# A convolution kernel's first step: stream sums on TensorE, a reordered set-up, and a split last store

## The chip, the cores and the metric

The kernel runs on one core of one Trainium2 chip. The metric is the device time of one execution in microseconds (us). The profile's span is about 2 us shorter than that time.

## The reference

A causal convolution over time with eight taps, each a full 512 x 512 matrix:

```python
x: (8, 4096, 512), kernel: (8, 512, 512)
for k in range(8):
    shifted = x moved k steps later in time, zeros in front
    out += np.matmul(shifted, kernel[k])
```

## The kernel before

Each of the 128 partitions owns a run of 256 consecutive time steps. A step of the kernel handles eight of them, so there are 32 steps. Within a step the eight taps are combined by a three-level scheme of sums and differences, which needs 27 matrix products in place of 64: three nodes (LO, HI, MID) of nine products each. A product is four accumulating matmuls of 128 x 128 by 128 x 512. The scheme needs

- **streams**: sums of x rows at several distances (`D4`, `D42`, `D421`, `D41`, and `F1`, `F2`, `F21` for the very first step), which are the stationary operands, and
- **weight differences** (`mid_a`, `mid_b`, `mid_c`): 19 combinations of the eight taps, 128 x 2048 each, made once. A product can start only when its weight is there.

The first step also needs the **history**: the seven rows ahead of each run, which belong to the neighbouring partition. Before the change the set-up was:

```python
    nc.vector.memset(D421, 0.0)
    xi = [load_x(0, 0)]                       # first half of x, step 0
    for b in range(B):                        # history, 8 pieces of 15 partitions
        nc.gpsimd.dma_start(out=D421[b*G+1:(b+1)*G, 1:8], in_=xr[...])
    for tap in (6, 4, 7, 5): load_w(tap)
    xi.append(load_x(0, 1))                   # second half of x, step 0
    for tap in (2, 0, 3, 1): load_w(tap)
    ...
        transpose_pe(T, xi[0], range(0, 4))   # TensorE, then ScalarE copies to XT
        transpose_pe(H, D421, range(0, 8))    # history
        tt(D4[:, 5:8], H[:, 1:4], hs[:, 1:4], ADD)      # VectorE makes all sums
        tt(D4[:, 0:4], hs, XT[:, 0:4], ADD)
        ...                                   # five weight differences
        transpose_pe(T, xi[1], range(4, 8))   # ahead of every product
        ...                                   # F1, F2, F21, the HI streams
    for k in range(4): ...                    # matmuls of zero into the four bank pairs
```

Every node then runs `node_a1` (one product and a ScalarE copy), `node_a0u` (two products), `node_seed` (ScalarE copies that seed the output banks), `node_v` (two products with VectorE's combination), four times `node_l` (the last products) and `node_e` (the output). In these traces each engine takes its work in the order of the program; e2 shows it for TensorE, with a wait of 4.0 us.

## Time and profile before

| | before |
|---|---|
| device time, median of 3 | 796.1 us |
| span of the profile | 793.6 us |
| TensorE busy | 760.0 us |
| VectorE's first sum | 18.4 us |
| first product on TensorE | 32.3 us |
| first `node_l` of node 2 on TensorE | 62.6 us |
| last matmul ends | 788.7 us |

The row that matters most is the last but one. From there to the end TensorE is full in both kernels (the last matmul ends 726.0 us later before the change, 726.1 us after it), so all that the change can win at the start is how much earlier that product comes. I call this instant **the marker**: in the timeline of TensorE it is the group of `F` matmuls which follows the four with `D` that are node 3's first product. In the kernel before it is the second of these lines (start, duration, engine; `x8` counts the matmuls; the bracket is the wait ahead of the group and what ended it):

```profile
61.42 1.03 PE L217 MATMUL qq<-w,D 128*128 128x512 bf16 x4
62.63 1.89 PE L217 MATMUL pp<-w,F 128*128 128x512 bf16 x8 [0.18 <-DVE pp L82]
```

The other lines behind the table stand in the prediction below.

### The profile page before, as it was taken

How to read it: one execution, taken by the hardware profiler on the slowest of the kernel's cores; microseconds unless marked ns; L12 is line 12 of the kernel's file. 1: busy time of each engine (PE TensorE's matmuls, PEld its weight loads, DVE VectorE, ACT ScalarE, POOL GpSimd, SP SyncE). 2: the span in 40 equal slices, each digit the busy share in tenths (PEclk: the TensorE clock that was granted, in tenths of full speed). 3: DMA queues.
4: the chain of work that ended last, by engine and by line, in shares of the span. 5: the costliest groups of instructions: out<-in, count | busy, mean ns of one | idle time of the engine just before them, and what ended most of it. 6: DMA issues, size and time to landing. Idle time of an engine off the chain costs nothing.

```text
span 793.6 us, 9335 instructions
## 1 busy us (share of the span) xinstructions
PE 760.0 (96%) x3528; PEld 345.7 (44%) x3528; DVE 662.3 (83%) x762; ACT 277.6 (35%) x455; POOL 44.7 (6%) x86
## 2 busy tenths in 40 slices
PE   2579999999999999999999999999999999999997
PEld 2224444444444444444444444444444444444443
DVE  1989898888888888889888888988888879888895
ACT  2233323333333333333333333333333333333332
POOL 6000000000000000000000000000000000000000
PEclk9999999999999999999999999999999999999999
DMA  9936777787878778778878877787778777878842
GB/s 153 209 52 177 186 173 178 169 203 167 206 160 188 170 175 183 188 172 189 192 164 176 188 193 169 182 176 176 175 188 207 156 190 171 174 188 184 192 137 121
DMA packets 161132, 138.83 MB, mean 175 GB/s; under 512 B 132296, under 2 KB 136392, under 8 KB 161088
## 3 DMA queue, kind: packets, MB, share of 16 engines
q1 hardware_dynamic: 147392, 99.63, 46.1%
q0 software_dynamic: 13696, 38.61, 30.4%
q8 instruction: 27, 0.44, 0.2%
q14 instruction: 17, 0.14, 0.1%
HBM read 77.22 MB, written 67.11 MB: 182 GB/s over the span
## 4 chain that ended last, share of the span: by engine, by line
PE 94%; DMA 2%; DVE 2%; ACT 1%; issue 0%; POOL 0%; ACTq 0%
PE pp L217 62%; PE qq L217 31%; DMA xin<-in_x_dram 2%; DVE w L82 1%; DMA D<-in_x_dram 1%; POOL w L143 0%; PE pp L208 0%; PE xt L167 0%; ACT XT L188 0%; DVE D L135 0%; ACT pp L259 0%; DVE y L82 0%; ACT qq L247 0%; PE qq L208 0%; DVE pp L271 0%
## 5 line engine op out<-in xcount | busy, mean ns | idle before, releaser
L217 PE MATMUL pp<-w,D 128*128 128x512 bf16 x2280 | 523.4, 379 | 1.4 <-ACT pp L259 1.3
L217 PEld LDWEIGHTS <-D 128*128 128x128 bf16 x3296 | 322.5, 98 | 394.5 <-issue 6.5
L217 PE MATMUL qq<-w,D 128*128 128x512 bf16 x1016 | 251.2, 380 | 1.4 <-ACT qq L247 1.4
L82 DVE TENSOR_TENSOR D<-D 128x1024 bf16<-128x1024 bf16 (+1 forms) x256 | 232.0, 947 | 0.1
L82 DVE TENSOR_TENSOR y<-pp,ms 128x1024 f32<-128x1024 f32 x124 | 151.4, 1221 | 47.9 <-PE pp L217 47.9
L82 DVE TENSOR_TENSOR D<-XT 128x2048 bf16<-128x2048 bf16 (+2 forms) x157 | 146.6, 950 | 7.6 <-DMA XT<-xin 6.3
L247 ACT COPY qq<-qq 128x512 f32<-128x512 f32 x96 | 54.7, 570 | 267.3 <-PE qq L217 267.3
L259 ACT COPY pp<-qq 128x512 f32<-128x512 f32 x96 | 54.7, 570 | 177.1 <-PE qq L217 172.7
L82 DVE TENSOR_TENSOR pp<-dts,pp 128x512 f32<-128x512 f32 x96 | 66.4, 692 | 51.5 <-ACT dts L263 47.2
L294 ACT COPY ms<-pp 128x1024 f32<-128x1024 f32 x62 | 63.0, 1016 | 34.2 <-PE pp L217 34.2
L87 POOL DMA_DIRECT2D xin<-in_x_dram x64 | 34.0, 532 | 699.0 <-DMA XT<-xin 688.1
L271 DVE SCALAR_TENSOR_TENSOR pp<-pp,dts 128x512 f32<-128x512 f32 x96 | 66.8, 695 | 3.6
L263 ACT COPY dts<-qq 128x512 f32<-128x512 f32 x96 | 58.2, 606 | 0.0
L261 ACT ACTIVATE pp<-qq 128x512 f32<-128x512 f32 x96 | 56.6, 590 | 0.1
L217 PE MATMUL qq<-w,XT 128*128 128x512 bf16 x124 | 31.8, 379 | 0.0
L82 DVE TENSOR_TENSOR w<-w,w 128x2048 bf16<-128x2048 bf16 x19 | 22.4, 1219 | 0.2
L167 PE MATMUL xt<-ident,xin 128*128 128x128 bf16 x32 | 3.8, 312 | 15.4 <-DMA xin<-in_x_dram 15.4
L217 PEld LDWEIGHTS <-XT 128*128 128x128 bf16 x124 | 12.1, 98 | 14.6
L82 DVE TENSOR_TENSOR D<-hist,D 128x1536 bf16<-128x1536 bf16 x1 | 1.0, 957 | 15.1 <-ACT D L175 15.1
L167 PEld LDWEIGHTS <-xin 128*128 128x128 bf16 x32 | 3.2, 146 | 15.7 <-DMA xin<-in_x_dram 15.7
L167 PE MATMUL hist<-ident,D 128*128 128x128 bf16 x32 | 3.8, 313 | 4.1 <-DMA D<-in_x_dram 4.1
L217 PEld LDWEIGHTS <-F 128*128 128x128 bf16 x36 | 3.3, 97 | 9.5 <-DVE w L82 4.8
(28 smaller groups left out, 51.4 us busy)
## 6 DMA issues: line engine op xcount, KB each, us to landing
out_dram<-y SPq DMA_DIRECT2D x128, 512.0 KB, 3.3
xin<-in_x_dram POOLq DMA_DIRECT2D x64, 512.0 KB, 6.0
w<-in_kernel_dram POOLq DMA_DIRECT2D x8, 512.0 KB, 13.9
XT<-xin SPq DMA_TRANSPOSE x62, 6.1
D<-in_x_dram POOLq DMA_DIRECT2D x8, 105.0 KB, 5.1
```

The source lines that it names most:

```text
L82: nc.vector.tensor_tensor(out=o, in0=a, in1=b, op=op)
L87: nc.gpsimd.dma_start(out=xin, in_=xr[:, K * i + 4 * h:K * i + 4 * h + 4, :])
L167: nc.tensor.transpose(o[:, t, c * P:(c + 1) * P], src[:, t % src.shape[1], c * P:(c + 1) * P], ident)
L217: nc.tensor.matmul(bank, lhsT=comp[:, c * P:(c + 1) * P], rhs=w[:, c, :], start=start and c == 0, stop=c == DC - 1, skip_group_check=True)
L247: nc.scalar.copy(out=n.q[:, 0], in_=n.q[:, 1])
L259: nc.scalar.copy(out=n.p[b_][:, 1], in_=n.q[:, 1])
L261: nc.scalar.mul(out=n.p[b_][:, 1], in_=n.q[:, 1], mul=-1.0)
L263: nc.scalar.copy(out=n.dts, in_=n.q[:, 0])
L271: nc.vector.scalar_tensor_tensor(out=p[:, 0], in0=p[:, 1], scalar=-1.0, in1=n.dts, op0=MUL, op1=SUB)
L294: nc.scalar.copy(out=ms[b_], in_=p)
```

## The change

The intent: let products begin before the second half of x has landed; take sums off VectorE by letting TensorE add while it transposes (two matmuls with an identity into one bank); take two weight differences off VectorE (one matmul with the identity, one with its negative); release TensorE's clock early with matmuls on zero (in the kernel before its matmuls take 0.43 us each until 34.2 us, then 0.216); load the history in two large transfers; and finish the last output pair in halves, stored from two queues. Cut to its core:

```diff
-    nc.vector.memset(D421, 0.0)
-    xi = [load_x(0, 0)]
-    for b in range(B): ... 15 rows of history each
+    nc.gpsimd.dma_start(out=H[1:P, 4:8], in_=xr[0:P - 1, RUN - 4:RUN, :])
+    x0 = [load_x(0, 0)]
+    nc.gpsimd.dma_start(out=H[1:P, 1:4], in_=xr[0:P - 1, RUN - 7:RUN - 4, :])
+    make_identity(nc, ident)          # also identh (batch starts zeroed), identn (negative)
+    nc.vector.memset(H[0:1], 0.0)
...
+    for r in range(2):
+        for k in range(4):
+            fill(pair(k))             # 16 matmuls on zero
+    o = transpose_pe(x0[0], 0)
+    nc.scalar.copy(out=XT[:, 0:4], in_=o)
+    pw = sums_pe(1, (-4, 0), (-3, 1))
+    nc.vector.tensor_copy(out=D4[:, 0:2], in_=pw)
...                                   # the other D4 parts, F1, F2, F21 in the same way
     nodes = [node_a1(0)]
     node_a0u(nodes[0])
     node_seed(nodes[0])
+    o = transpose_pe(x0[1], 2)        # second half of x only here
     node_v(nodes[0], 0)
     node_v(nodes[0], 1)
...
+                by_pe(*mid_a(LO, HI), (2, 0))
...
+                by_pe(*mid_a(HI, HI), (1, 0))
...
+            if b_ == HI and n.k == len(order) - 1:
+                for j, eng in enumerate((nc.scalar, nc.sync)):
+                    tt(y[:, j], p[:, j], ms[b_][:, j], ADD if n.a == LO else SUB)
+                    eng.dma_start(out=orr[:, ... + j, :], in_=y[:, j])
```

More of the change, by code (lines that the diff above doesn't have):

```diff
@@ L54 @@
     ctx.enter_context(tc.manual_schedule())
-    ident = spool.tile([P, P], bf, name="ident")
-    make_identity(nc, ident)
-    zero = spool.tile([P, D], bf, name="zero")
-    nc.vector.memset(zero, 0.0)
     W = {}
@@ L74 @@
     D1 = spool.tile([P, 2, D], bf, name="D1")
-    F2 = spool.tile([P, 5, D], bf, name="F2")
+    F2 = spool.tile([P, 2, D], bf, name="F2")
     F21 = spool.tile([P, 4, D], bf, name="F21")
@@ L131, in prep_d421, with pair @@
             tt(D421[:, 4:8], D42[:, 3:7], D42[:, 4:8], ADD)
-    nc.vector.memset(D421, 0.0)
-    xi = [load_x(0, 0)]
-    for b in range(B):
-        nc.gpsimd.dma_start(out=D421[b * G + 1:(b + 1) * G, 1:8],
-                            in_=xr[b * G:(b + 1) * G - 1, RUN - 7:RUN, :])
+    ppool = ctx.enter_context(tc.tile_pool(name="p", bufs=1, space=PSUM))
+    def pair(k):
+        return ppool.tile([P, 2, D], f32, name=f"pp{k}")
+    H = D421
+    nc.gpsimd.dma_start(out=H[1:P, 4:8], in_=xr[0:P - 1, RUN - 4:RUN, :])
+    x0 = [load_x(0, 0)]
+    nc.gpsimd.dma_start(out=H[1:P, 1:4], in_=xr[0:P - 1, RUN - 7:RUN - 4, :])
+    ident = spool.tile([P, P], bf, name="ident")
+    make_identity(nc, ident)
+    identh = spool.tile([P, P], bf, name="identh")
+    nc.gpsimd.tensor_copy(out=identh, in_=ident)
+    nc.gpsimd.memset(identh[:, 0:P:G], 0.0)
+    identn = spool.tile([P, P], bf, name="identn")
+    nc.gpsimd.tensor_scalar_mul(out=identn, in0=ident, scalar1=-1.0)
+    zero = spool.tile([P, D], bf, name="zero")
+    nc.vector.memset(zero, 0.0)
+    nc.vector.memset(H[0:1], 0.0)
     def load_w(tap):
@@ L145, in mid_a, with by_dve, by_pe @@
     def mid_a(b_, c_):
-        tt(W[MID, b_, c_], W[HI, b_, c_], W[LO, b_, c_], SUB)
+        return W[MID, b_, c_], W[HI, b_, c_], W[LO, b_, c_]
     def mid_b(a, c_):
-        tt(W[a, MID, c_], W[a, HI, c_], W[a, LO, c_], SUB)
+        return W[a, MID, c_], W[a, HI, c_], W[a, LO, c_]
     def mid_c(a, b_):
-        tt(W[a, b_, MID], W[a, b_, LO], W[a, b_, HI], SUB)
+        return W[a, b_, MID], W[a, b_, LO], W[a, b_, HI]
+    def by_dve(o, u, v):
+        tt(o, u, v, SUB)
+    def by_pe(o, u, v, prs):
+        for h in range(2):
+            pw = pair(prs[h])
+            for k in range(2):
+                nc.tensor.matmul(pw[:, k], lhsT=ident, rhs=u[:, 2 * h + k], start=True, stop=False)
+                nc.tensor.matmul(pw[:, k], lhsT=identn, rhs=v[:, 2 * h + k], start=False, stop=True)
+            nc.scalar.copy(out=o[:, 2 * h:2 * h + 2], in_=pw)
@@ L154 @@
     for tap in (6, 4, 7, 5):
         load_w(tap)
-    xi.append(load_x(0, 1))
+    x0.append(load_x(0, 1))
     for tap in (2, 0, 3, 1):
         load_w(tap)
-    with tc.tile_pool(name="t", bufs=1, space=PSUM) as tpool:
-        H = tpool.tile([P, K, D], bf, name="hist")
-        T = tpool.tile([P, K, D], bf, name="xt0")
-        def transpose_pe(o, src, ts_):
-            for t in ts_:
-                for c in range(DC):
-                    nc.tensor.transpose(o[:, t, c * P:(c + 1) * P],
-                                        src[:, t % src.shape[1], c * P:(c + 1) * P], ident)
-        transpose_pe(T, xi[0], range(0, 4))
-        transpose_pe(H, D421, range(0, 8))
-        nc.scalar.copy(out=XT[:, 0:4], in_=T[:, 0:4])
-        nc.scalar.copy(out=F0, in_=T[:, 0])
-        hs = D421[:, 4:8]
-        nc.scalar.copy(out=hs, in_=H[:, 4:8])
-        tt(D4[:, 5:8], H[:, 1:4], hs[:, 1:4], ADD)
-        tt(D4[:, 0:4], hs, XT[:, 0:4], ADD)
-        prep_d41(LO)
-        mid_b(LO, HI)
-        tt(D42[:, 7], D4[:, 5], D4[:, 7], ADD)
-        prep_d42(LO)
-        mid_c(LO, LO)
-        prep_d421(LO)
-        mid_b(LO, LO)
-        mid_c(LO, MID)
-        mid_c(LO, HI)
-        transpose_pe(T, xi[1], range(4, 8))
-        nc.scalar.copy(out=XT[:, 4:8], in_=T[:, 4:8])
-        tt(F1[:, 0], hs[:, 3], XT[:, 0], ADD)
-        tt(F1[:, 1], XT[:, 0], XT[:, 1], ADD)
-        tt(F2[:, 0], hs[:, 1], hs[:, 3], ADD)
-        tt(F2[:, 1:3], hs[:, 2:4], XT[:, 0:2], ADD)
-        tt(F2[:, 3:5], XT[:, 0:2], XT[:, 2:4], ADD)
-        tt(F21, F2[:, 0:4], F2[:, 1:5], ADD)
-        prep_d4(HI)
-        prep_d41(HI)
-        prep_d42(HI)
-        prep_d421(HI)
-        prep_d27()
@@ L200, with fill, transpose_pe @@
-    xi = [load_x(1, 0), load_x(1, 1)]
-    ppool = ctx.enter_context(tc.tile_pool(name="p", bufs=3, space=PSUM))
-    qpool = ctx.enter_context(tc.tile_pool(name="q", bufs=1, space=PSUM))
-    for k in range(4):
-        pw = ppool.tile([P, 2, D], f32, name="pp") if k else qpool.tile([P, 2, D], f32, name="qq")
+    def fill(pw):
         for h in range(2):
             nc.tensor.matmul(pw[:, h], lhsT=ident, rhs=zero, start=True, stop=True)
+    def transpose_pe(src, k):
+        o = pair(k).bitcast(bf).rearrange("p a (b d) -> p (a b) d", b=2)
+        for t in range(4):
+            for c in range(DC):
+                nc.tensor.transpose(o[:, t, c * P:(c + 1) * P], src[:, t, c * P:(c + 1) * P], ident)
+        return o
@@ new lines, in x_at, with sums_pe @@
+    def x_at(t):
+        return (x0[0][:, t], ident) if t >= 0 else (H[:, 8 + t], identh)
+    def sums_pe(k, *sums):
+        pw = pair(k)
+        for h, ts_ in enumerate(sums):
+            for c in range(DC):
+                for n, t in enumerate(ts_):
+                    src, idt = x_at(t)
+                    nc.tensor.matmul(pw[:, h, c * P:(c + 1) * P], lhsT=src[:, c * P:(c + 1) * P],
+                                     rhs=idt, start=n == 0, stop=n == len(ts_) - 1,
+                                     skip_group_check=True)
+        return pw
@@ new lines @@
+    for r in range(2):
[5 more added lines that the diff above has]
+    nc.vector.tensor_copy(out=D4[:, 0:2], in_=pw)
+    pw = sums_pe(2, (-2, 2), (-1, 3))
+    nc.vector.tensor_copy(out=D4[:, 2:4], in_=pw)
+    pw = sums_pe(3, (-5, -1))
+    nc.vector.tensor_copy(out=D4[:, 7], in_=pw[:, 0])
+    pw = sums_pe(0, (-7, -3), (-6, -2))
+    nc.scalar.copy(out=D4[:, 5:7], in_=pw)
@@ new lines @@
+    prep_d41(LO)
+    pw = sums_pe(1, (-1, 0), (0, 1))
+    nc.scalar.copy(out=F1, in_=pw)
+    fill(pair(3))
+    tt(D42[:, 7], D4[:, 5], D4[:, 7], ADD)
+    prep_d42(LO)
+    pw = sums_pe(2, (-2, 0), (0, 2))
+    nc.scalar.copy(out=F2, in_=pw)
+    pw = sums_pe(0, (-3, -2, -1, 0), (-2, -1, 0, 1))
+    nc.scalar.copy(out=F21[:, 0:2], in_=pw)
+    by_dve(*mid_b(LO, HI))
+    pw = sums_pe(1, (-1, 0, 1, 2), (0, 1, 2, 3))
+    nc.scalar.copy(out=F21[:, 2:4], in_=pw)
+    nc.scalar.copy(out=F0, in_=XT[:, 0])
@@ L210 @@
+    fill(pair(0))
+    fill(pair(1))
+    prep_d421(LO)
+    by_dve(*mid_c(LO, LO))
+    by_dve(*mid_b(LO, LO))
+    by_dve(*mid_c(LO, MID))
+    by_dve(*mid_c(LO, HI))
+    xi = [load_x(1, 0)]
     mpool = ctx.enter_context(tc.tile_pool(name="m", bufs=2))
@@ L226, in streams @@
         if a == MID and i == 0:
-            return (F0, [F1[:, 0], F1[:, 1]], [F2[:, 1], F2[:, 3]],
+            return (F0, [F1[:, 0], F1[:, 1]], [F2[:, 0], F2[:, 1]],
                     [F21[:, j] for j in range(4)])
@@ L234, in streams, with node_a1 @@
                 [D421[:, o + j] for j in range(4)])
-    def node_a1(i, a):
+    def node_a1(k):
         n = Node()
-        n.i, n.a, n.s = i, a, streams(i, a)
-        n.q = qpool.tile([P, 2, D], f32, name="qq")
+        n.k, (n.i, n.a) = k, order[k]
+        a = n.a
+        n.s = streams(n.i, a)
+        n.q = pair(3)
         product(n.q[:, 1], n.s[1][1], W[a, MID, HI], True)
@@ L256, in node_seed @@
         for b_ in range(2):
-            n.p[b_] = ppool.tile([P, 2, D], f32, name="pp")
+            n.p[b_] = pair((2 * n.k + b_) % 3)
             if b_ == LO:
@@ L296, in node_e @@
             y = ypool.tile([P, 2, D], f32, name="y")
-            if n.i == 0:
+            if b_ == HI and n.k == len(order) - 1:
+                for j, eng in enumerate((nc.scalar, nc.sync)):
+                    tt(y[:, j], p[:, j], ms[b_][:, j], ADD if n.a == LO else SUB)
+                    eng.dma_start(out=orr[:, K * n.i + 4 * n.a + 2 * b_ + j, :], in_=y[:, j])
+            elif n.i == 0:
                 nc.scalar.copy(out=y, in_=p)
@@ L306 @@
     order += [(i, a) for i in range(1, NIT) for a in (MID, LO, HI)]
-    nodes = [node_a1(*order[0])]
+    nodes = [node_a1(0)]
     node_a0u(nodes[0])
     node_seed(nodes[0])
+    o = transpose_pe(x0[1], 2)
     node_v(nodes[0], 0)
     node_v(nodes[0], 1)
+    nc.scalar.copy(out=XT[:, 4:8], in_=o)
+    xi.append(load_x(1, 1))
+    prep_d4(HI)
+    prep_d41(HI)
+    by_dve(*mid_b(HI, HI))
+    prep_d42(HI)
     for k, (i, a) in enumerate(order):
@@ L324 @@
             if k == 0:
-                mid_b(HI, HI)
-                mid_c(HI, LO)
-                mid_b(HI, LO)
-                mid_c(HI, MID)
-                mid_c(HI, HI)
-                nodes.append(node_a1(*order[1]))
-            else:
-                mid_a(LO, HI)
-                mid_a(HI, HI)
-                mid_b(MID, HI)
-                mid_a(LO, LO)
-                mid_a(HI, LO)
-                mid_b(MID, LO)
-                mid_c(MID, MID)
-                mid_c(MID, LO)
-                mid_c(MID, HI)
-                nodes.append(node_a1(*order[2]))
-            node_e(cur, 1)
+                by_pe(*mid_a(LO, HI), (2, 0))
+                node_e(cur, 1)
+                fill(pair(2))
+                nodes.append(node_a1(1))
+                by_pe(*mid_a(HI, HI), (1, 0))
+                prep_d421(HI)
+                by_dve(*mid_b(HI, LO))
+                by_dve(*mid_c(HI, MID))
+                by_dve(*mid_c(HI, LO))
+                by_dve(*mid_c(HI, HI))
+                by_dve(*mid_b(MID, HI))
+                by_dve(*mid_a(LO, LO))
+                prep_d27()
+            else:
+                by_dve(*mid_a(HI, LO))
+                by_dve(*mid_b(MID, LO))
+                by_dve(*mid_c(MID, MID))
+                by_dve(*mid_c(MID, LO))
+                by_dve(*mid_c(MID, HI))
+                nodes.append(node_a1(2))
+                node_e(cur, 1)
         nxt = nodes[k + 1] if k + 1 < len(order) else None
@@ L374 @@
             node_l(cur, 1, HI)
-        if 1 <= k and k + 2 < len(order):
-            nodes.append(node_a1(*order[k + 2]))
+        if k and k + 2 < len(order):
+            nodes.append(node_a1(k + 2))
         if k >= 2:
```

## The prediction

> **What bounds the kernel now.** I read the page's busy shares and groups first, then the chain that ended last, then the timeline of the first 70 us and the last 15 us. The page says where the bulk lies:
>
> ```profile
> PE 760.0 (96%) x3528; PEld 345.7 (44%) x3528; DVE 662.3 (83%) x762; ACT 277.6 (35%) x455; POOL 44.7 (6%) x86
> PE   2579999999999999999999999999999999999997
> L217 PE MATMUL pp<-w,D 128*128 128x512 bf16 x2280 | 523.4, 379 | 1.4 <-ACT pp L259 1.3
> ```
>
> TensorE is full from the fourth slice (each is 19.8 us) to the end; 1.4 us of idle in 2280 matmuls. A busy mean of 379 ns counts overlap: 1391 matmuls start in the 300 us from 100 to 400, so one costs 0.2157 us. There are 96 nodes x 9 products x 4 = 3456 of them: 745.5 us at that pace. The last ends at 788.66, so 43.2 us are lost before and between, nearly all at the start. The change leaves the 3456 alone; it can win only part of those 43 us and of the 4.9 us after 788.66. The chain over the first 70 us, start and duration ahead of each piece:
>
> ```profile
> 7.97 0.78 POOL w L143
> ...
> 11.14 13.86 DMA xin<-in_x_dram
> 25.00 0.05 issue
> 25.05 1.90 PE xt L167 x16
> ...
> 28.89 1.01 PE qq L208 x2
> 29.90 2.56 PE pp L208 x6
> 32.46 1.72 PE qq L217 x4
> ...
> 49.65 2.27 DVE w L82 x2
> 51.92 0.02 issue
> 51.95 3.51 DVE w L82 x3
> ...
> 61.89 0.70 DVE pp L82
> ```
>
> The reader sees that no product starts before 32.3 us, because the second half of the first x tile (landed 25.0) is transposed ahead of all products, and that from 49 us TensorE waits for VectorE's weight differences. The four matmuls from 32.46 take 0.43 us each, twice 0.2157; from 34.87 they run at full pace. The page's clock row does not show this. VectorE in that stretch (start, duration, engine):
>
> ```profile
> 18.41 0.96 DVE L82 TENSOR_TENSOR D<-hist,D 128x1536 bf16<-128x1536 bf16 x1 [15.13 <-ACT D L175]
> 39.95 5.88 DVE L82 TENSOR_TENSOR w<-w,w 128x2048 bf16<-128x2048 bf16 x5
> 49.56 10.67 DVE L82 TENSOR_TENSOR w<-w,w 128x2048 bf16<-128x2048 bf16 x9
> ```
>
> It idles 15.1 us, starts at 18.4 and then runs to 62.6 with about 4 us of gaps: some 40 us of work. **The start is a VectorE chain that begins late**; at 62.63 TensorE takes over as bound.
>
> **The skill.** "TensorE: Matmul & The Clock Gate", Part 1, says the array starts at half clock and is released after about 3.4 us of sustained work (free-running window); the trace agrees in kind: 0.43 us a matmul until 34.2, after 5.3 us of matmuls, then 0.216. Part 4 of that page says transposes do not count as busy for the gate, and Part 2 gives about 81 ns for a sustained N=128 load-and-matmul pair; the trace only has the slow ones, 16 transposes in 1.90 us. "VectorE: DVE Perf Modes", the perf-mode tier table: a bf16 tensor_tensor of 2048 takes 1224 ns, which the trace shows (1.22), and an fp32 PSUM operand drops to 1x, which 1.22 us for 1024 elements of the y additions shows. "DMA: Bandwidth & Descriptors", Issuing engines are not separate DMA queues: a second queue saves only issue time.
>
> **Part 1, loads.** The history goes from eight 15-row transfers behind a 1.76 us memset to two of 127 rows issued first. The queue then moves 0.52 MB at about 2.4 us (0.524 MB at 218 GB/s, as between 18 and 34 us). Before, the weight taps landed near 15.2, 18.0, then some 2.35 us apart, x half two at 25.0. After, I estimate x half one 8.0, second history 9.8, taps 12.2, 14.6, 17.0, 19.4, x half two 21.8, taps 24 to 31.4. Nobody waits on the later ones below.
>
> **Part 2, TensorE before the products.** The identity is ready after three POOL issues of 0.67 and some 0.7 us: 3.4. Then 16 fills on zero: 12 slow (5.2 us) and 4 quick (0.9) end at 9.5. Then 16 transposes and four groups of sums (16, 16, 8, 16 small matmuls), later 96 more for F1, F2, F21 with 6 fills. I take 0.07 us each, between half of the 0.118 measured and the skill's 0.081: transposes done at 10.7, sums at 11.9, 13.0, 13.6, 14.7, all at 14.7 + 6.7 + 1.3 = 22.7.
>
> **Part 3, VectorE.** Removed: the D4 additions from history (0.96 + 1.22), seven F additions (3 x 0.42 + 0.69 + 0.68 + 1.23 = 3.9), two weight differences now on TensorE (2.4). Added: three PSUM copies (1.2 + 1.2 + 0.69). Work to the first node_l of node 2 falls from 40 to about 37 us. It now starts at 11.9. Step by step: copies to 15.0, D41 15.7, D42 17.3, mid_b 18.5, D421 19.8, four mids 24.5. TensorE: first product 23.6, ScalarE's copy 24.2, eight matmuls 26.0, transposes of half two 27.1, node_v 28.0. So VectorE waits 3.5 us here, then 28.0 to 29.6 for both node_v; the D preparations and mid_b(HI,HI) to 35.0, four mids 39.7, two more and D27 42.5, node_v 43.8, five mids 49.7, prep_m 51.5, node_v(2) 52.2. Before, the same point is 62.58. **Gain 10.4 us.** The 16 difference matmuls (16 x 0.216 = 3.5 us) lie inside TensorE's waits for VectorE between 30 and 43.
>
> **Part 4, tail.** Before: addition 788.69 to 789.92, one 512 KB store, its data at 400 GB/s gone by 792.0, end 793.6. After: the scheduled order has only the first half-addition waiting for TensorE and the second not, so the first waits for the whole pair. Halves of 0.69 end at 789.4 and 790.0; the second store's 256 KB take 0.64 us in place of 1.28. **Gain 0.6 us**, from halving the last store, not from the second queue.
>
> Sum: 796.1 - 10.4 - 0.6 = 785.1; I say 785.
>
> **Rivals.** (1) The small matmuls stay at the slow pace (0.118): 168 of them cost 8 us more, TensorE's preamble ends near 30, and the gain shrinks to 3 or 4: 792. The fills speak against it, the transposes' not counting speaks for it. (2) Small pairs at 0.056 and an early clock release: VectorE's 3.5 us wait nearly goes and the copies start by 11: 782. (3) Transfers are the bound: products then follow the weight landings, which gain only some 3 us over before: 793. Against it: VectorE's order uses each tap later than my landing estimate, the tightest being tap 1, 31.4 against 36. (4) The second step's x transposes do not come earlier, and TensorE waits near 55 for what it gains at 50; before they were ready by 43.9 and not waited for at 60, so I give this little.
>
> **Range and chances.** Rivals 1 and 3 pull to 788 and beyond, rival 2 to 782; ten per cent each side gives 781.5 to 788.5. Over 2% faster needs 780.2, which needs the wait at node 0 to vanish, and more; 0.06. Slower by 2% has no mechanism; 0.01.
>
> **What would show it.** In the changed profile: fills from about 3.5 to 9.5 with a change from 0.43 to 0.22 us; small matmuls near 0.07 us each; VectorE's first copy at 12; its wait before node_v(0) about 3.5 us; first node_l of node 2 at about 52; from there the same 0.2157 us pace; last matmul at about 778.3, and 4.3 us after it. Wrong if VectorE's first copy is past 14, if a transfer ends a TensorE wait after 25, or if TensorE shows idle time between 55 and 100.

## The result, and the profile after

The changed kernel took **786.59 us** (median of 5, 786.18 to 787.32) against 796.76 us for the kernel before in the same rounds. The ratio is 0.9872, 95% interval 0.9854 to 0.9890: faster, by less than 2%. A ratio here is the mean time of one kernel's fast runs over that of the other's in the same rounds, so it is not quite the ratio of the medians.

The groups of the page show the changed kernel as before in the bulk, with more TensorE work inside a shorter span (the last line counts more matmuls than before because the banks once named `qq` are now `pp` too):

```profile
span 784.1 us, 9632 instructions
PE 770.0 (98%) x3680; PEld 352.7 (45%) x3680; DVE 658.2 (84%) x756; ACT 284.4 (36%) x463; POOL 42.7 (5%) x83
PE   8889999999999999999999999999999999999997
L251 PE MATMUL pp<-w,D 128*128 128x512 bf16 x3296 | 719.0, 379 | 3.2 <-DVE pp L77 1.2
```

The first slices rise from 2, 5, 7 tenths to 8, 8, 8. TensorE is busy 10 us more (152 additional small and other matmuls), yet the span is 9.5 us shorter: the additional work lies in what were waits. VectorE's timeline of the start (start, duration, engine; the bracket is the wait ahead of the group and what ended it):

```profile
11.88 1.23 DVE L214 CAST D<-pp 128x1024 bf16<-128x1024 f32 x1 [8.64 <-PE pp L203]
19.55 1.23 DVE L77 TENSOR_TENSOR w<-w,w 128x2048 bf16<-128x2048 bf16 x1 [0.18 <-DMA w<-in_kernel_dram]
22.10 3.62 DVE L77 TENSOR_TENSOR w<-w,w 128x2048 bf16<-128x2048 bf16 x3 [1.32 <-DMA w<-in_kernel_dram]
27.53 0.70 DVE L77 TENSOR_TENSOR pp<-dts,pp 128x512 f32<-128x512 f32 x1 [1.80 <-PE pp L251]
35.11 7.03 DVE L77 TENSOR_TENSOR w<-w,w 128x2048 bf16<-128x2048 bf16 x6 [0.50 <-DMA w<-in_kernel_dram]
```

VectorE starts at 11.9 in place of 18.4, but it now waits three times for a weight tap (0.18, 1.32, 0.50: 2.0 us), which it never did before. The chain that ended last, over the first 80 us, says the same ("issue" is time in which the engine waited for nothing that the profile shows):

```profile
4.58 9.43 DMA w<-in_kernel_dram
14.02 0.28 issue
14.30 20.72 DMA w<-in_kernel_dram
35.02 0.03 issue
...
36.37 4.73 DVE w L77 x5
...
43.13 4.49 PE pp L251 x20
```

Up to 35.0 us it consists of transfers, then of VectorE's differences, then of TensorE. The wait with which it passes from the last tap to VectorE is only 0.50 us: the two are near balance there. TensorE's timeline leads to the marker:

```profile
43.13 3.61 PE L251 MATMUL pp<-w,D 128*128 128x512 bf16 x16 [1.23 <-DVE pp L77]
48.32 1.89 PE L251 MATMUL pp<-w,F 128*128 128x512 bf16 x8 [0.71 <-ACT pp L283]
50.87 1.89 PE L251 MATMUL pp<-w,F 128*128 128x512 bf16 x8 [0.66 <-ACT pp L295]
52.59 1.03 PE L251 MATMUL pp<-w,D 128*128 128x512 bf16 x4
53.45 1.89 PE L251 MATMUL pp<-w,F 128*128 128x512 bf16 x8
```

The marker is at 53.45 in place of 62.63, **9.2 us earlier**. The last matmul ends at 779.56 in place of 788.66, 9.1 us earlier: nothing was given back on the way. The tail, after before:

```profile
788.69 1.23 DVE L82 TENSOR_TENSOR y<-pp,ms 128x1024 f32<-128x1024 f32 x1 [0.50 <-PE pp L217]
```

```profile
779.59 1.29 DVE L77 TENSOR_TENSOR y<-pp,ms 128x512 f32<-128x512 f32 x2 [0.50 <-PE pp L251]
780.31 0.37 ACTq L337 DMA_DIRECT2D out_dram<-y  x1
780.90 0.33 SPq L337 DMA_DIRECT2D out_dram<-y  x1
```

From the last matmul to the end of the span it is 4.94 us before (793.6 - 788.66) and 4.54 after (784.1 - 779.56), so the tail gives 0.4 us. 9.1 + 0.4 is the 9.5 us between the spans. The profiles of e3 to e7, e9, e11 and e12 have 4.46 to 4.55 us here, those of e2 and e10 6.3 (see there); of the kernel before there is one.

### The profile page after: what moved, and what is told of

The parts are those of the page before. It is cut to its first block, busy times and chain, and to the rows that moved or that the text cites. A ratio compares the mean times of both kernels' runs of the same rounds, so it can differ in the third digit from the quotient of the medians.

```text
span 784.1 us, 9632 instructions
## 1 busy us (share of the span) xinstructions
PE 770.0 (98%) x3680; PEld 352.7 (45%) x3680; DVE 658.2 (84%) x756; ACT 284.4 (36%) x463; POOL 42.7 (5%) x83
## 4 chain that ended last, share of the span: by engine, by line
PE 92%; DMA 4%; DVE 2%; issue 1%; POOL 0%; ACT 0%; DVEq 0%; ACTq 0%; POOLq 0%
PE pp L251 92%; DMA w<-in_kernel_dram 4%; DVE w L77 1%; DVE y L77 1%; DVE D L77 0%; DVE pp L77 0%; ACT pp L295 0%; POOL D L136 0%; DVE pp L307 0%; DVEq L459 0%; ACT pp L283 0%; POOL D L138 0%; POOL identn L146 0%; POOL ident masks.py:199 0%; POOL identh L143 0%
## 5 line engine op out<-in xcount | busy, mean ns | idle before, releaser
L251 PE MATMUL pp<-w,D 128*128 128x512 bf16 x3296 | 719.0, 379 | 3.2 <-DVE pp L77 1.2
L77 DVE TENSOR_TENSOR y<-pp,ms 128x1024 f32<-128x1024 f32 (+1 forms) x125 | 151.5, 1213 | 47.6 <-PE pp L251 47.5
L283 ACT COPY pp<-pp 128x512 f32<-128x512 f32 x96 | 54.8, 570 | 260.1 <-PE pp L251 260.1
L295 ACT COPY pp<-pp 128x512 f32<-128x512 f32 x96 | 54.7, 570 | 175.2 <-PE pp L251 171.2
L330 ACT COPY ms<-pp 128x1024 f32<-128x1024 f32 x62 | 63.0, 1016 | 34.2 <-PE pp L251 34.2
L299 ACT COPY dts<-pp 128x512 f32<-128x512 f32 x96 | 58.0, 604 | 0.0
L297 ACT ACTIVATE pp<-pp 128x512 f32<-128x512 f32 x96 | 56.5, 589 | 0.1
L251 PE MATMUL pp<-w,XT 128*128 128x512 bf16 x124 | 31.8, 379 | 0.0
L184 PE MATMUL pp<-zero,ident 128*128 128x512 bf16 x24 | 8.8, 519 | 4.5 <-POOL ident masks.py:199 3.6
L251 PE MATMUL pp<-w,F 128*128 128x512 bf16 x36 | 8.7, 379 | 1.4 <-ACT pp L283 0.7
L203 PE MATMUL pp<-ident,xin 128*128 128x128 bf16 x80 | 7.5, 219 | 0.0
L203 PE MATMUL pp<-identh,D 128*128 128x128 bf16 x72 | 6.9, 219 | 0.0
```

Source lines behind the costliest of these rows:

```text
L77: nc.vector.tensor_tensor(out=o, in0=a, in1=b, op=op)
L184: nc.tensor.matmul(pw[:, h], lhsT=ident, rhs=zero, start=True, stop=True)
L203: nc.tensor.matmul(pw[:, h, c * P:(c + 1) * P], lhsT=src[:, c * P:(c + 1) * P], rhs=idt, start=n == 0, stop=n == len(ts_) - 1, skip_group_ ...
L251: nc.tensor.matmul(bank, lhsT=comp[:, c * P:(c + 1) * P], rhs=w[:, c, :], start=start and c == 0, stop=c == DC - 1, skip_group_check=True)
L283: nc.scalar.copy(out=n.q[:, 0], in_=n.q[:, 1])
L295: nc.scalar.copy(out=n.p[b_][:, 1], in_=n.q[:, 1])
```

## The experiments

My theory was that the start is a chain of VectorE work and weight transfers, in which each part of the change counts only so far as no other wait takes it up. The rivals: the transfers alone set it, or TensorE itself. Twelve runs followed: e2 to e5, e11 and e12 undo one part of the changed kernel, e6 leaves two loads out, e7, e8 and e10 go further, e1 puts the tail alone on the kernel before, and e9 repeats the changed kernel. The table sums them up; "marker" and "last matmul" are from the profile of each, and the details follow.

| run | median us | ratio to before | marker | last matmul |
|---|---|---|---|---|
| changed kernel | 786.59 | 0.9872 | 53.45 | 779.56 |
| e1 tail alone, on the kernel before | 796.66 | 1.0003 | 65.41 | 791.44 |
| e2 x half two first | 792.88 | 0.9951 | 58.20 | 784.39 |
| e3 sums on VectorE | 787.64 | 0.9891 | 54.64 | 781.08 |
| e4 differences on VectorE | 789.77 | 0.9921 | 56.97 | 783.31 |
| e5 no opening fills | 786.81 | 0.9868 | 53.73 | 779.91 |
| e6 no history loaded (wrong result) | 783.39 | 0.9826 | 50.05 | 776.24 |
| e7 node 2's first product earlier | 787.47 | 0.9879 | 52.76 | 778.87 |
| e8 first half-addition earlier | 788.28 | 0.9889 | 53.63 | 781.00 |
| e9 changed kernel again | 786.77 | 0.9865 | 54.64 | 780.73 |
| e10 e7 and VectorE reordered | 786.03 | 0.9858 | 52.76 | 778.85 |
| e11 last store on one queue | 786.5 (one run) | | 53.78 | 779.89 |
| e12 loads as before | 788.59 | 0.9888 | 54.73 | 780.95 |

**e9, the base, and what makes runs differ.** The changed kernel unaltered, on the chip of e5 to e12.

> The changed kernel once more, as a base on the same chip for the next. Expected: 786 to 788 us, first node_l of node 2 near 53.5, and in the executions that are slower by 1 us or more a granted clock below 1.000, because TensorE's short waits before 60 us let the clock fall.

It took 786.77 us, but its profiled execution has the marker at 54.64, 1.2 us later than the first profile. TensorE's timeline of e9, ahead of node 0's second products:

```profile
23.79 1.04 PE L251 MATMUL pp<-w,D 128*128 128x512 bf16 x4 [1.81 <-DVE w L77]
25.05 1.87 PE L251 MATMUL pp<-w,D 128*128 128x512 bf16 x4 [0.22 <-DVE w L77]
26.71 1.84 PE L190 MATMUL pp<-ident,xin 128*128 128x128 bf16 x16
```

In the first profile the same four matmuls take 1.02 us and the 16 transposes 1.06. Here the clock fell to half after a wait of 1.8 us, stayed there until about 28.4 and so moved everything by up to 2 us, of which VectorE's later waits took up 0.8. Over 20 to 40 us the clock row gives 0.91 for e9. So the start of this kernel has a random part of a microsecond or two. The stretches of e2, e3 and e4 show it too (0.91, 0.83, 0.88), and e1 ran most of some 20 matmuls at half clock between 57 and 65. That is most of the 2.8 us by which its marker is late: ahead of them it was 0.5 us behind the kernel before. The expectation that slow executions have a mean clock below 1.000 held only in part: two of 787.3 us had 0.998 and 1.000.

**e2, the order of the transposes.**

```diff
+    o = transpose_pe(x0[1], 2)
+    nc.scalar.copy(out=XT[:, 4:8], in_=o)
     nodes = [node_a1(0)]
     node_a0u(nodes[0])
     node_seed(nodes[0])
-    o = transpose_pe(x0[1], 2)
     node_v(nodes[0], 0)
     node_v(nodes[0], 1)
-    nc.scalar.copy(out=XT[:, 4:8], in_=o)
```

> The changed kernel, but the second half of the first x tile is transposed ahead of the first product again. Theory (in-order TensorE then waits for that half, landing near 24.5): the first product moves from 21.5 to about 25.6, VectorE's first node_v from 27.5 to about 30.5, and the whole costs 2.5 to 3 us. Rival (weight transfers alone set the start, tap 1 at 35.0): VectorE catches up in its waits for transfers and the cost is under 0.7 us.

TensorE's timeline of e2:

```profile
25.40 1.51 PE L190 MATMUL pp<-ident,xin 128*128 128x128 bf16 x16 [4.02 <-DMA xin<-in_x_dram]
26.70 1.91 PE L251 MATMUL pp<-w,D 128*128 128x512 bf16 x4
```

The marker moved by 4.75 us, more than expected. The mechanism is the expected one, TensorE held by a transfer that the next product does not need, but after the 4.0 us wait the clock also fell: the first product ran at half pace (1.91 us for four). From the start of the transposes to ScalarE's copy of the product 3.3 us passed; in the changed kernel the two take 0.9 and 1.1 us. So about 1.4 us of the 4.75 are the clock's and some 3.4 the order's own (an estimate from these lines). VectorE's `node_v` came at 33.1 in place of 27.5. The timed runs are 6.3 us slower; 1.8 us more than the changed kernel's tail passed after the last matmul in this profile, where the two last stores landed in 4.0 us in place of 2.1 and 2.2. Why is open; e10's profile shows the same without this edit (6.35 us, 4.0 us), so it does not belong to the order. The rival (under 0.7 us) is out. **This reordering is a third to a half of what the change gains.**

**e3, the sums.** TensorE only transposes the history (one matmul with `identh` for each row and chunk), ScalarE copies it out, and VectorE adds, as in the kernel before.

```diff
-    pw = sums_pe(1, (-4, 0), (-3, 1))
-    nc.vector.tensor_copy(out=D4[:, 0:2], in_=pw)
-    ...
+    pw = sums_pe(1, (-4,), (-3,))
+    nc.scalar.copy(out=hb[:, 0:2], in_=pw)
+    ...
+    tt(D4[:, 0:4], hb[:, 0:4], XT[:, 0:4], ADD)
+    tt(D4[:, 5:8], ha[:, 1:4], hb[:, 1:4], ADD)
+    ...                                # F1, F2, F21 by tt, behind mid_c(LO, HI)
```

> The changed kernel, but the history is only transposed by TensorE and the sums (D4, F1, F2, F21) are made by VectorE, as before the change. Theory (VectorE's work sets the start): D4 is ready some 3 us later and VectorE has some 3 us more to do, of which its waits of 2.0 us for transfers and 1.8 us for TensorE take up some; cost 4 to 6 us. Rival (the start is bound by the weight transfers): under 1.5 us.

Against the first profile it cost 1.2 us at the marker, and about 1 us in time; against e9, whose clock dipped as this one's did, the marker is the same (54.64). Either way it is the rival's figure, though not by the rival's reason alone. VectorE's timeline of e3:

```profile
14.21 1.23 DVE L77 TENSOR_TENSOR D<-w,XT 128x2048 bf16<-128x2048 bf16 x1 [10.96 <-ACT w L217]
21.03 4.75 DVE L77 TENSOR_TENSOR w<-w,w 128x2048 bf16<-128x2048 bf16 x4
28.03 1.23 DVE L77 TENSOR_TENSOR F<-F 128x2048 bf16<-128x2048 bf16 x1
29.52 0.70 DVE L77 TENSOR_TENSOR pp<-dts,pp 128x512 f32<-128x512 f32 x1 [0.27 <-PE pp L252]
```

VectorE starts 2.3 us later than with the sums on TensorE, and has the F sums to do (25.70 to 29.26). But the four weight differences no longer wait for their taps (they end at 25.8, as in the changed kernel at 25.7), and the F sums fill the time in which it waited for TensorE; `node_v` is 2.0 us later, and the 0.5 us wait for the last tap is absorbed as well. The sums that give the change its name are worth at most about 1 us here, because VectorE had waits to hold the work. (The clock dip of this profile costs little in the comparison with the first: TensorE made VectorE wait 0.27 us.)

**e4, the two differences on TensorE.**

```diff
-                by_pe(*mid_a(LO, HI), (2, 0))
-                by_pe(*mid_a(HI, HI), (1, 0))
+                by_dve(*mid_a(LO, HI))
+                by_dve(*mid_a(HI, HI))
                 by_dve(*mid_b(MID, HI))
```

> The changed kernel, but the two weight differences that it makes on TensorE are back on VectorE (2 x 1.18 us, after tap 1 has landed). Theory (after tap 1 lands at 35.0 the chain is VectorE's): node_v of node 1 moves from 42.4 to 44.7, cost 2.0 to 2.4 us. Rival (TensorE itself has become the bound, and it loses 16 matmuls or 3.5 us): same or up to 1 us faster.

VectorE's timeline of e4:

```profile
36.25 9.41 DVE L77 TENSOR_TENSOR w<-w,w 128x2048 bf16<-128x2048 bf16 x8
```

The group is 2.38 us longer than the six of the changed kernel (7.03) and starts 1.14 later, which is the clock dip of this profile. Together they are the marker's 3.5 us; so the part itself is 2.4 us, at the upper end of the expectation; against e9's marker, with its own dip, it is 2.3. The timed runs (789.8) contain such dips too (clock 0.992 to 0.996). TensorE's 3.5 us of additional matmuls were hidden: that rival is out.

**e5, the fills.** The loop of 16 matmuls on zero is deleted.

> The changed kernel without its 16 opening fills. Theory (they only release TensorE's clock early): the first transposes start at 9.5 in place of 9.9 but the small matmuls cost 0.107 us in place of 0.056 for several us, VectorE's first copy is near 13 in place of 11.9, the D4 sums are 2 us later, of which its waits for taps 7 and 5 take up 1.5; cost 0.5 to 2 us. Rival (the clock stays down through the small matmuls): preamble some 8 us longer, cost 4 us or more.

VectorE's first copy came at 12.92 in place of 11.88, and its waits for the two taps shrank from 1.50 to 1.02 us. The marker moved by 0.3 us, the time by nothing that can be measured (786.81). That is below the expected 0.5 to 2: one microsecond was lost and mostly taken up. The trace shows what the fills do: without them the 16 transposes and the first 20 matmuls of the sums started some 0.107 us apart, and from 13.1 us on, 3.8 us after the first of them, 0.056 us. These small matmuls release the clock themselves, only later, and the rival is out.

**e12, the loads.**

```diff
-    nc.gpsimd.dma_start(out=H[1:P, 4:8], in_=xr[0:P - 1, RUN - 4:RUN, :])
+    nc.vector.memset(H, 0.0)
+    make_identity(nc, ident)
     x0 = [load_x(0, 0)]
-    nc.gpsimd.dma_start(out=H[1:P, 1:4], in_=xr[0:P - 1, RUN - 7:RUN - 4, :])
+    for b in range(B):
+        nc.gpsimd.dma_start(out=H[b*G+1:(b+1)*G, 1:8], in_=xr[...])
```

> The changed kernel with the loads as before the change: identity first, x, then the history in eight pieces behind a full memset. Theory (the new loads bring the history earlier but not the weights, as the transfers ran at the same 205 GB/s before): VectorE's first copy at 14 to 15 in place of 11.9, of which its waits for taps 7 and 5 take up most; first node_l of node 2 later by 0.3 to 1.5 us. Rival (the loads carry a large part of the gain): 3 us or more.

As expected: first copy at 14.37, marker 1.3 us later than in the first profile (neither has a clock dip), time about 2 us more (788.59 against 786.77 on the same chip). The POOL queue shows when the first tap landed, because its last weight issue waits for it: 14.3 in the changed kernel, 15.3 here, 15.2 before the change. TensorE's sums waited 3.1 us for the history here and began at 13.26; in the changed kernel they began at 10.79 without a wait. So the new loads bring the history at least 2.5 us earlier and the first tap 1 us.

**e6, how much the transfers hold up.** Wrong (relative error 0.11): the history's two loads are removed and `H` is zeroed.

> Wrong result on purpose: the changed kernel with the history left at zero and its two loads (0.91 MB) taken out, so every tap lands about 4 us earlier and nothing else changes. Theory (VectorE's three waits for taps, 2.0 us in all, lie on the path): they vanish and the time falls by 1.5 to 2 us. Rival A (the waits are slack, TensorE or VectorE work sets the end anyway): under 0.4 us. Rival B (the start is bound by the transfers throughout): 3.5 us or more.

VectorE's timeline of e6:

```profile
9.68 1.23 DVE L212 CAST D<-pp 128x1024 bf16<-128x1024 f32 x1 [6.42 <-PE pp L201]
17.09 4.75 DVE L77 TENSOR_TENSOR w<-w,w 128x2048 bf16<-128x2048 bf16 x4
24.71 0.70 DVE L77 TENSOR_TENSOR pp<-dts,pp 128x512 f32<-128x512 f32 x1 [2.87 <-PE pp L249]
31.71 7.02 DVE L77 TENSOR_TENSOR w<-w,w 128x2048 bf16<-128x2048 bf16 x6
```

The waits for taps are gone and the marker is 3.4 us earlier, more than the 2.0 us of waits and just short of rival B. The experiment was not as clean as I meant it: x landed earlier as well, the identity was ready 1.1 us earlier and the fills took 5.3 us in place of 6.4. So the transposes behind them began at 7.7 in place of 9.9, VectorE's first copy moved by 2.2 us, and VectorE then waited 2.9 us for TensorE. To the marker, e6's chain that ended last holds no transfer at all, only engines' work: the identity, the fills, and what follows them. Had the transposes begun at 9.9, that chain would be 2.2 us later and the gain about 1.2 (an estimate). So 3.4 us is what leaving the two loads out is worth at the start, and by that estimate the landing of the taps is the smaller part of it. The transfers are on the changed kernel's path, as its own chain shows; in the kernel before the chain ran through one too, the second half of x (13.86 us), but through no tap.

**e7, e10: beyond the change.** In e7 the first product of node 2 is issued between the two halves of node 1's last products, where its ScalarE copy is covered. e10 adds a later place for two VectorE instructions that node 1 does not need.

```diff
+        if k == 1:
+            nodes.append(node_a1(2))
         if k < 2:
             node_l(cur, 1, LO)
...
-                nodes.append(node_a1(2))
                 node_e(cur, 1)
# e10 also: mid_a(LO, LO) to node 1's differences, prep_d27 behind them
```

> The changed kernel with the first product of node 2 issued between the two pairs of node 1, so that ScalarE's copy of it (0.7 us wait at 47.6) is covered. Theory (TensorE is the bound from 43 us on, with two such waits): the last matmul comes 0.7 to 1.0 us earlier. Rival (VectorE's chain still sets it): nothing, the wait moves to VectorE's node_v of node 2 at 52.0.

> The changed kernel with two more moves: the first product of node 2 goes between node 1's pairs, and two VectorE instructions that node 1 does not need (one weight difference, D27) go behind node 1's node_v. Theory (after tap 1 lands, waits of TensorE for VectorE and ScalarE set the start): first node_l of node 2 at 52.2 to 52.8 in place of 53.5, 0.7 to 1.2 us less. Rival (VectorE's total work sets it, so the order moves nothing): 53.4 or later.

e7 has the marker 0.7 us earlier (52.76) and the last matmul too (778.87). e10 has the same 52.76, although node 1's `node_v` comes 1.1 us earlier than in e7; its timeline of TensorE shows the new wait:

```profile
51.21 1.03 PE L251 MATMUL pp<-w,D 128*128 128x512 bf16 x4
52.76 1.89 PE L251 MATMUL pp<-w,F 128*128 128x512 bf16 x8 [0.52 <-DVE pp L77]
```

VectorE's work is then the bound to the instant, so the rival was half right: order wins 0.7 us, no more. The timed runs of e10 (785.43 to 787.28) against e9's (786.09 to 787.35) overlap, and those of e7 (785.49 to 788.33) say nothing. As a candidate that beats the changed kernel too, e10 does so by 0.7 us in the medians and at the marker, not clear of the noise. Its profiled execution is the slowest of its four, with the long tail that e2 showed (6.35 us).

**e1, e8, e11: the tail.** e1 puts the split last store on the kernel before; e11 issues both halves from one queue; e8 places the first half-addition ahead of the last product in program order.

```diff
# e11
-                for j, eng in enumerate((nc.scalar, nc.sync)):
+                for j, eng in enumerate((nc.sync, nc.sync)):
# e8
+        if k == len(order) - 1:
+            half(cur, 0, y=cur.y)     # first half: addition and store
         if k >= 2:
             node_l(cur, 1, HI)
```

> The kernel before with the change's tail alone. Theory (the start gives nearly all): last matmul stays near 788.7, and what follows it shrinks from 4.9 us to about 4.5, so about 0.4 us in all (796). Rival (the tail is worth more than its share, through the second queue): 2 us or more.

> The changed kernel with both halves of the last store on the one queue of the SyncE. Theory (the tail's 0.4 us come from halving the last store): from last matmul to end 4.5 to 4.6 us, as with two queues. Rival (the second queue matters): 4.9 or more.

> The changed kernel with the first half of the last addition placed ahead of the last product in program order, so that it waits for its own bank only. Theory (in the changed kernel both halves wait for the whole pair): the first half starts about 0.5 us before the last matmul ends, the second right after it; from last matmul to end 4.5 becomes 4.0 us. Rival (the last store's fixed time is all that counts): nothing.

e1 is the same as the kernel before within 0.2% (1.0003, 0.9983 to 1.0024), so 2 us or more are out; 0.4 cannot be seen in times, and its profile has 4.8 us after the last matmul, 0.2 less than before and not 0.4. e11 needs 4.5 us from last matmul to end (779.89 to 784.4), as with two queues: the second queue does nothing measurable, which agrees with the Trainium skill, "DMA: Bandwidth & Descriptors", Issuing engines are not separate DMA queues. e8 failed in an instructive way. Its timeline of TensorE at the end:

```profile
775.73 3.19 PE L251 MATMUL pp<-w,D 128*128 128x512 bf16 x14
779.96 1.02 PE L251 MATMUL pp<-w,D 128*128 128x512 bf16 x4 [1.05 <-DVE y L77]
```

What follows the last matmul did shrink, to 3.7 us (784.7 - 781.00). But the last product, which writes the other bank of the same tile, now waited 1.05 us for VectorE's reading of the first bank. The wait was only turned around. Making the two banks two tiles might avoid this; that was not tried.

## Why the prediction was right

785 us was forecast, within 781.5 to 788.5; 786.59 was measured.

**The bound and the path** held. VectorE's chain set the start: its first copy was forecast at 11.9 and came at 11.88; `node_v` of node 0 at 28.0 (27.53), of node 1 at the end of D27, 42.5 (42.39), node 1's five differences done at 49.7 (49.51), `node_v` of node 2 done at 52.2 (52.70). From the marker on the pace was unchanged; TensorE's one wait between 55 and 100 us was 0.17 us for ScalarE, none for the second step's x, so rival 4 did not come.

**Part 1 was wrong in size, and the sentence "Nobody waits on the later ones" fell.** The estimate started the queue too early and let it run at 218 GB/s. The first tap landed at 14.3 (forecast 12.2), tap 5 at 22.1 (19.4), tap 1 at 35.0 (31.4): eight transfers in 20.7 us, 2.6 us each. VectorE waited 2.0 us for them. That did not show in the total, because a second error had the other sign: I gave TensorE 0.07 us a small matmul and VectorE a wait of 3.5 us for it; they took 0.056 us (72 of them in 4.02 us in e6), the first product came at 21.5 in place of 23.6, and VectorE waited 1.8 us for TensorE. So the transfers took the place of a TensorE wait; that the two errors nearly cancel is luck. Rival 1 (0.118 us) is out. Rival 2 had the pace right (0.056 us), but the taps took up what it frees. Rival 3 named the right resource with too large a price.

Three slips in the working: between 18 and 34 us the kernel before moved 199 to 216 GB/s in stretches of 2 us, 207 in the mean and not 218; the removed F additions are six, not seven (their sum is right); and the terms listed in part 3 take about 5.4 us off VectorE, not the 3 of "from 40 to about 37" (the traces show 40.6 and 35.9 us busy). The 10.4 us rests on the step-by-step count, not on the last two.

**The gain at the marker, 10.4 forecast, was 9.2.** For VectorE it was 9.9 (62.58 to 52.70), 0.5 less than the sum. The rest was lost because at the marker VectorE was no longer the later of the two: TensorE had waited 0.71 and 0.66 us for ScalarE's copies of node 2 and still had node 3's first product to do. The step that failed is the reading "before, the same point is 62.58" on VectorE alone. e7 takes 0.7 us of it back.

**The fills and the removed sums** were counted as parts of VectorE's earlier start and lighter load. e3 and e5 show that they mattered little (at most 1.2 us, and 0.3 us), since waits stood ready to hold what they remove; the reordering (e2: 4.75, of it some 1.4 by the clock), the two differences (e4: 2.4) and the loads (e12: 1.3) carry the change. The five sum to 9.9, near the 9.2 of the whole; they need not be equal, as waits are shared.

**The tail** gave 0.4 in place of 0.6 (0.2 in e1). Half-additions end 0.7 and 1.3 us after the last matmul as forecast, both wait for the pair, and the second queue does not count (e11), which leaves the cause named, the halved store.

## What to carry to other kernels

When several engines and the transfers are near balance in a start-up, count a removed piece of work only after asking which wait stands ready to take it up; undoing one part at a time showed that the headline part was at most an eighth of the gain and one moved line a third to a half of it. Profile the base twice: its marker moved by 1.2 us between two executions, as much as some of the parts are worth. On an engine that works in program order, nothing that waits for a late transfer should stand ahead of work whose operands are there. And follow every engine to the last instant before the steady state: the bound can change hands there.

## What the Trainium skill lacked or had wrong

- "TensorE: Matmul & The Clock Gate", Why this matters for your kernels, asks for no idle gaps above about 3 us. Read alone that is too wide: in e9 a wait of 1.81 us with another of 0.22 was followed by half clock (four matmuls in 1.87 us), and in e4 one of 1.60 (1.78 us). In e8 and e10 waits of 1.78 and 1.73 us at the same place were not, so the length of one gap did not decide it. (The page's passage on PSUM-queue cycling does allow for short gaps, without a figure.)
- The same page, Part 2, gives about 81 ns for a sustained N=128 load-and-matmul pair. Here 72 pairs took 4.02 us (e6), 56 ns each, which is the page's figure for isolated matmuls.
- The same page, Part 4, says that the full clock doesn't engage for transposes. Behind the fills, 16 transposes started 0.89 us before the next matmul (9.90 to 10.79), 56 ns each: once released by other matmuls, the clock serves them too. In e5 transposes and the sums behind them released it together, 3.8 us after the first transpose; whether transposes alone would was not tested.
